# A second layer in twelve rounds per head pair, with the last block's projections spread over its eight periods

## The chip, the cores and the metric

The kernel runs on one core of a Trainium2 chip. The time is the device time of one execution in microseconds. TensorE (PE) does the matrix products, VectorE (DVE), ScalarE (ACT) and GpSimd (POOL) the elementwise work, SyncE (SP) issues all DMAs here.

## What is computed

One step of a two-layer encoder on 2048 prompt tokens and 8 running streams of 16 tokens, model width 1024, in fp32. Layer 1 is a gated delta rule; layer 2, which the change concerns, is RWKV-7 time mixing with 16 heads of 64. The core of layer 2 in the reference:

```python
xs = h[None] + xx[None] * mu[:, None, None, :]
rkvz = jnp.einsum('gbtd,dge->gbte', xs[:4], w_in.reshape(D, 4, W_B)).astype(f32)
r, k, v, z = rkvz[0], rkvz[1], rkvz[2], rkvz[3]
def step(S, inp):
    r_t, w_t, k_t, v_t, a_t, b_t = inp
    sa = jnp.einsum('bhvk,bhk->bhv', S, a_t)
    S = S * w_t[:, :, None, :] + sa[..., None] * b_t[:, :, None, :] + v_t[..., None] * k_t[:, :, None, :]
    return S, jnp.einsum('bhvk,bhk->bhv', S, r_t)
```

The scan's output is normalised per head, a bonus term (the sum of r k r_k, times v) is added, it is multiplied by the SiLU gate of z and goes through the output projection; a last RMSNorm follows. Both layers start with an RMSNorm.

## The kernel before

**Tiling.** Layer 2 has six blocks (`B_BLOCKS`): the first of two 64-token chunks and the 8 x 16 sample tokens, then five of 384 tokens, which are six chunks. A block has eight head pairs (`KT`), so there are 48 pairs. Head pairs are handled in 54 **periods**: period i takes pair i through its preparation, and earlier pairs through later stages.

**Stages of a pair**, each a Python generator whose `yield` ends a step:

- `b_prep` (period i): two low-rank products (L1050), the elementwise work on DVE, ACT and POOL, the key norms (L1114), the bonus product (L1123, kept in `bv`), the masked chunk products (L1138, masked by DVE at L1143 into `GM`), and at the end `N`, written to DRAM (`scrb`) and read back as `B`.
- `b_subst` (period i + 1): a forward substitution of 15 steps of two small DVE instructions each (L776, L778), then two transfers through DRAM (`sc2b`, `cm`).
- `b_inverse` (period i + 2): POOL spreads `cm` into T (L1195), then products L1211 (three times), L1225, L1240, L106, L1259, and L1272 with L1275; T is updated between them by DVE, ACT and POOL.
- `b_scan` (period i + 3): for each chunk a product px (L1309), copied to `XV` by ACT (L1312, L1313); then L1316, the product pu (L1320), and L1325. DVE makes the next chunk's XV from pu (L1322) and the state R (L1323). So L1309 of a chunk needs L1322 of the one before. Sample tokens have products of their own (L1339 to L1364). `b_centre` subtracts the mean into `OC`.
- `b_gate` (in the period of the scan): group norm of OC (POOL scales it at L1402), a turn of OC by PE (L106, a helper's line), bonus and SiLU gate on DVE (L1411, L1412), and the split into `oh` and `ol` (L162, L163).
- `b_out` (every other period, for two pairs): eight output products of six matmuls each (L168 to L170) with weights `whl` from DRAM in two buffers. `b_final` is the last norm of a block (`norm_scale`, L204 and L205).

**The stream.** Beside the pairs a generator `b_stream` computes the projections of the blocks, one block and more ahead: 136 **units** per block, each of six 128 x 384 matmuls (L991 to L993) with one weight pair (six buffers, loaded at L133). Results go to DRAM (`kvd`), and `b_load` fetches K, R and V of a pair. A period takes `PACE` = 17 units; 101 were taken ahead of the first period, so that the stream ends in period 43, and periods 44 to 53 have no unit.

**What sets the order.** PE's instructions stand in the order in which the code is recorded (`MANUAL`). In a period `weave` sets it: each part has a number of steps and a stretch (a, b) of the period, and the part whose next step lies earliest goes on. The other engines' queues and SyncE's are sorted by a scheduler after due times that are taken from PE's order (`_due`).

```python
parts.append((self.b_scan(*at(i - 3)), 16, 0.1, 0.8))
parts.append((self.b_subst(*at(i - 1)), 15, 0.0, 0.55))
parts.append((self.b_gate(*at(i - 3)), 4, 0.7, 1.0))
parts.append((islice(st, PACE), PACE, 0.0, 1.0))
```

## Time and profile before

| | |
|---|---|
| median of three runs (lowest to highest) | 4778.23 us (4771.09 to 4779.44) |
| the profiled execution | 4774.21 us, its span 4772.5 us |
| busy share of the span | PE 93%, PE's weight loads 79%, DVE 72%, ACT 48%, POOL 36% |
| granted TensorE clock over the span | 0.954 of full speed |
| layer 2, from its first L1050 to the end | 2498 to 4772.5 us |
| first pair of blocks 1 and 2 | L1050 at 2806 and 3198 us |
| first pair of the last block | L1050 at 4340 us |

The table by stage gives for each stretch the busy time of each engine (with its number of instructions), the granted clock (PEclk, 1.00 is 2.4 GHz, 0.50 is 1.2 GHz), the DMA engines' share and GB/s. In a timeline, the brackets behind an instruction say how long its engine stood idle ahead of it and what ended that.

### The profile page before, as it was taken

What the parts mean: (1) busy time and instruction counts of PE and PEld (TensorE: products, weight loads), DVE (VectorE), ACT (ScalarE), POOL (GpSimd) and SP (SyncE); (2) the same over time, 40 slices, a digit from 0 to 9 for tenths busy, and PEclk for the clock granted to TensorE, in tenths of its full rate; (3) what the DMA queues carried; (4) which work ended last, traced back from release to release, by engine and by line L of the source; (5) the groups of instructions that cost most, each with busy time, mean ns of one, the idle gap of its engine ahead of it and who ended that gap; (6) DMA issues with size and microseconds to landing.
All of it is one profiled execution on the core that took longest, in us unless ns stands there. A gap on an engine that the chain in (4) does not pass through costs nothing.

```text
span 4772.5 us, 103994 instructions
## 1 busy us (share of the span) xinstructions
PE 4427.8 (93%) x37093; PEld 3776.5 (79%) x37093; DVE 3446.9 (72%) x9156; ACT 2307.5 (48%) x6197; POOL 1730.0 (36%) x2507
## 2 busy tenths in 40 slices
PE   6899999999999999999887988989999999999976
PEld 6778788878888899999886766878877877787765
DVE  5777866686666766766778888777776776777674
ACT  4544544454444444444475565554554454455442
POOL 5555443332111211111115454444443343343441
PEclk9999999999999999999998989999999999999987
DMA  6655665565555676676555666746656665665432
GB/s 196 193 178 184 214 214 176 171 190 174 155 142 158 177 210 178 190 217 182 167 174 171 221 203 208 223 145 197 193 168 182 175 189 169 174 196 154 129 85 63
DMA packets 767975, 845.33 MB, mean 177 GB/s; under 512 B 263736, under 2 KB 499664, under 8 KB 767456
## 3 DMA queue, kind: packets, MB, share of 16 engines
q1 hardware_dynamic: 767456, 838.68, 59.3%
q8 instruction: 293, 4.80, 0.4%
q14 instruction: 226, 1.85, 0.1%
HBM read 635.88 MB, written 202.53 MB: 176 GB/s over the span
## 4 chain that ended last, share of the span: by engine, by line
PE 64%; DVE 19%; ACT 5%; issue 4%; DMA 4%; POOL 3%; SPq 0%; POOLq 0%; DVEq 0%; ACTq 0%
PE ps L390 6%; PE ps L392 6%; PE ps L391 6%; PE ps L991 5%; PE ps L168 4%; PE ps L169 4%; PE ps L992 4%; PE ps L993 4%; PE ps L170 4%; DVE sbt L776 2%; DVE cv L505 2%; PE ps L1320 2%; DVE TB L778 2%; PE ps L1309 1%; PE ps L106 1%
## 5 line engine op out<-in xcount | busy, mean ns | idle before, releaser
L390 PE MATMUL ps<-hh,whl 128*128 128x384 f32 (+1 forms) x1960 | 798.4, 407 | 10.4 <-ACT hh L162 8.2
L392 PE MATMUL ps<-hh,whl 128*128 128x384 f32 (+1 forms) x1960 | 715.2, 365 | 3.5 <-POOL whl L125 3.2
L391 PE MATMUL ps<-hl,whl 128*128 128x384 f32 (+1 forms) x1960 | 712.5, 364 | 1.8 <-DVE hl L163 1.5
L991 PE MATMUL ps<-xh,whl 128*128 128x384 f32 (+1 forms) x1632 | 623.7, 382 | 15.0 <-ACT whl L124 7.0
L992 PE MATMUL ps<-xl,whl 128*128 128x384 f32 (+1 forms) x1632 | 557.3, 341 | 17.3 <-POOL xl L163 12.7
L993 PE MATMUL ps<-xh,whl 128*128 128x384 f32 (+1 forms) x1632 | 555.2, 340 | 6.4 <-DVE whl L125 5.9
L125 POOL TENSOR_TENSOR whl<-wraw,whl 128x256 fp32r<-128x256 f32 x454 | 368.2, 816 | 416.9 <-ACT whl L124 390.7
L505 DVE SCALAR_TENSOR_TENSOR cv<-pre,cw,cv 128x512 f32<-128x512 f32 (+3 forms) x576 | 381.3, 669 | 137.2 <-ACT cv L503 130.9
L390 PEld LDWEIGHTS ps<-hh,whl 128*128 128x128 f32 x1960 | 375.5, 192 | 65.3 <-issue 16.4
L124 ACT CAST whl<-wraw 128x256 fp32r<-128x256 f32 x726 | 287.7, 404 | 261.4 <-PE ps L392 85.0
L392 PEld LDWEIGHTS ps<-hh,whl 128*128 128x128 f32 x1960 | 375.0, 191 | 41.8 <-POOL whl L125 7.2
L391 PEld LDWEIGHTS ps<-hl,whl 128*128 128x128 f32 x1960 | 376.1, 192 | 34.1 <-DVE hl L163 4.8
L168 PE MATMUL ps<-oh,whl 128*128 128x384 f32 (+2 forms) x1024 | 393.0, 384 | 9.4 <-ACT oh L162 4.1
L169 PE MATMUL ps<-ol,whl 128*128 128x384 f32 (+2 forms) x1024 | 366.3, 358 | 9.0 <-DVE ol L163 8.9
L991 PEld LDWEIGHTS ps<-xh,whl 128*128 128x128 f32 x1632 | 320.3, 196 | 64.6 <-ACT whl L124 8.5
L170 PE MATMUL ps<-oh,whl 128*128 128x384 f32 (+2 forms) x1024 | 364.4, 356 | 0.0
L778 DVE TENSOR_TENSOR TB<-TB,sbt 48x15 f32<-48x15 f32 (+14 forms) x1320 | 335.6, 254 | 19.7
L776 DVE TENSOR_TENSOR sbt<-B,TB 48x15 f32<-48x15 f32 (+14 forms) x1320 | 330.9, 251 | 25.2 <-DMA B<-scrb 3.2
L992 PEld LDWEIGHTS ps<-xl,whl 128*128 128x128 f32 x1632 | 322.5, 198 | 31.5 <-POOL xl L163 17.0
L993 PEld LDWEIGHTS ps<-xh,whl 128*128 128x128 f32 x1632 | 322.0, 197 | 10.9 <-DVE whl L125 10.4
L754 DVE TENSOR_TENSOR x<-x,ps 128x384 f32<-128x384 f32 (+1 forms) x320 | 191.2, 597 | 94.2 <-PE ps L170 91.2
L168 PEld LDWEIGHTS ps<-oh,whl 128*128 128x128 f32 x1024 | 199.2, 195 | 38.0 <-ACT oh L162 7.3
(342 smaller groups left out, 10365.4 us busy)
## 6 DMA issues: line engine op xcount, KB each, us to landing
whl<-wd SPq DMA_DIRECT2D x1582, 256.0 KB
wd<-whl SPq DMA_DIRECT2D x428, 256.0 KB
wraw<-in_w_a SPq DMA_DIRECT2D x288, 128.0 KB
wraw<-in_w_b SPq DMA_DIRECT2D x256, 128.0 KB
kvd<-kvo SPq DMA_DIRECT2D x160, 192.0 KB
xn<-x1d SPq DMA_DIRECT2D x80, 192.0 KB
wraw<-in_w_ao SPq DMA_DIRECT2D x96, 128.0 KB
xn<-in_x SPq DMA_DIRECT2D x48, 192.0 KB
```

Of the source, the lines that this page charges most:

```text
L168: self.nc.tensor.matmul(out, lhsT=wh, rhs=hh, start=first and i == 0, stop=False)
L169: self.nc.tensor.matmul(out, lhsT=wh, rhs=hl, start=False, stop=False)
L170: self.nc.tensor.matmul(out, lhsT=wl, rhs=hh, start=False, stop=i == n - 1)
L390: nc.tensor.matmul(p, lhsT=wh[:, k % 2], rhs=hh, start=k == 0, stop=False)
L391: nc.tensor.matmul(p, lhsT=wh[:, k % 2], rhs=hl, start=False, stop=False)
L392: nc.tensor.matmul(p, lhsT=wl[:, k % 2], rhs=hh, start=False, stop=k == KT - 1)
L505: nc.vector.scalar_tensor_tensor(o, f(j), self.cw[:, ct, j:j + 1], o, op0=MUL, op1=ADD)
L776: nc.vector.tensor_tensor(o, B[:, j + 1:16, j:j + 1].to_broadcast([rows, m, j + 1]), T[:, j:j + 1, 0:j + 1].to_broadcast([rows, m, j + 1]) ...
L778: nc.vector.tensor_tensor(T[:, j + 1:16, 0:j + 1], T[:, j + 1:16, 0:j + 1], o, op=SUB)
L991: nc.tensor.matmul(o, lhsT=wh[:, i], rhs=xh, start=k == 0, stop=False)
L992: nc.tensor.matmul(o, lhsT=wh[:, i], rhs=xl, start=False, stop=False)
L993: nc.tensor.matmul(o, lhsT=wl[:, i], rhs=xh, start=False, stop=k == KT - 1)
```

## The change

It replaces `weave` in layer 2 by `rounds`. A period has twelve rounds. Each part has a list of the rounds in which it makes a step, either written out or evenly spread over a stretch, and the parts are served in a fixed order in each round: prep, inverse, gate, substitution, scan, output products, last norm, stream. The scan makes one step in each round where it has twelve (2 per chunk, 6 for the sample tokens of the first block, spread over the period). The substitution takes rounds 1 to 8. The gate moves from the scan's period to the next one, rounds 1, 2, 3 and 6. The output products move to the second half of their period. `b_prep` has an empty step ahead of the norms and one ahead of the bonus product, and two fewer behind it. In the last eight periods of preparation (40 to 47) the stream takes 8 units (`LAST_PACE`) in place of 17. In `norm_scale` the mean square is taken from PSUM by one DVE instruction behind all products, where each column of up to three had its own. The `assert` lines add nothing to the program.

```diff
-AHEAD, PACE = 101, 17
+AHEAD, PACE, LAST_PACE, ROUNDS = 101, 17, 8, 12
...
                 nc.tensor.matmul(p1[0:w, c:c + 1], lhsT=acc[i][:, a:b], rhs=self.ones[:, 0:1], start=i == 0, stop=i == 1)
-            nc.vector.tensor_scalar(ms[0:w, 0, c:c + 1], p1[0:w, c:c + 1], 1.0 / D, 1e-6, op0=MUL, op1=ADD)
+        nc.vector.tensor_scalar(ms[:, 0, 0:len(spans)], p1[:, 0:len(spans)], 1.0 / D, 1e-6, op0=MUL, op1=ADD)
...
+    def rounds(n, parts):
+        live = []
+        for g, *at in parts:
+            if len(at) > 1:
+                k, a, e = at
+                at = [[max(1, math.ceil(n * (a + (e - a) * (i + 1) / k) - 1e-6)) for i in range(k)]]
+            live.append((g, list(at[0])))
+        for r in range(1, n + 1):
+            for p in list(live):
+                g, at = p
+                while p in live and ((at and at[0] <= r) or r == n):
+                    if at:
+                        at.pop(0)
+                    try:
+                        next(g)
+                    except StopIteration:
+                        live.remove(p)
...
+            if at(i):
+                parts.append((self.b_prep(*at(i)), range(1, 13)))
+            if at(i - 2):
+                parts.append((self.b_inverse(*at(i - 2)), (1, 2, 3, 4, 5, 6, 7, 8, 10)))
+            if at(i - 4):
+                parts.append((self.b_gate(*at(i - 4)), (1, 2, 3, 6)))
+            if at(i - 1):
+                parts.append((self.b_subst(*at(i - 1)), range(1, 9)))
             if at(i - 3):
-                parts.append((self.b_scan(*at(i - 3)), 16, 0.1, 0.8))
-            if at(i - 2):
-                parts.append((self.b_inverse(*at(i - 2)), 10, 0.0, 1.0))
+                b = at(i - 3)[0]
+                parts.append((self.b_scan(*at(i - 3)), 2 * b["ncp"] + 6 * b["nsc"], 0.0, 1.0))
...
-                    parts.append((out, 8, 0.0, 0.8))
+                    parts.append((out, 8, 0.5, 1.0))
                 else:
-                    parts.append((chain(out, self.b_final(blocks[j // KT])), 21, 0.0, 1.0))
+                    parts.append((chain(out, self.b_final(blocks[j // KT])), 21, 0.5, 1.0))
...
-            if at(i):
-                parts.append((self.b_prep(*at(i)), 12, 0.2 if i == 0 else 0.0, 1.0))
-            if at(i - 1):
-                parts.append((self.b_subst(*at(i - 1)), 15, 0.0, 0.55))
-            if at(i - 3):
-                parts.append((self.b_gate(*at(i - 3)), 4, 0.7, 1.0))
-            parts.append((islice(st, PACE), PACE, 0.0, 1.0))
-            self.weave(parts)
+            m = PACE if i < npair - KT else LAST_PACE
+            parts.append((islice(st, m), m, 0.0, 1.0))
+            self.rounds(ROUNDS, parts)
```

The lines of the changed kernel are shifted: L1309, L1316, L1320 and L1325 are L1334, L1341, L1345 and L1350, the units' L991 to L993 are L1014 to L1016, and L1211 is L1236.

**Scan and units.** PE's queue in period 28 (a middle block), from the scan's first pu product to the next chunk's px; before:

```order
L1316 MATMUL ps_49553<-R_30427,KR_47550 64x64 x2
L1320 MATMUL ps_49608<-XV_48884,TM_48883 64x64 x2
L1325 MATMUL ps_49553<-XV_48884,GM_47945 64x64 x2
L991 MATMUL ps_49404<-xh_49105,whl_49424 128x384
L992 MATMUL ps_49404<-xl_49106,whl_49424 128x384
L993 MATMUL ps_49404<-xh_49105,whl_49424 128x384
L991 MATMUL ps_49404<-xh_49112,whl_49424 128x384
L992 MATMUL ps_49404<-xl_49113,whl_49424 128x384
L993 MATMUL ps_49404<-xh_49112,whl_49424 128x384
L1309 MATMUL ps_49665<-XV_48884,GM_47945 64x64 x2
```

The same place in the changed kernel, where pu is in round 2 and the next px in round 3:

```order
L1341 MATMUL ps_49472<-R_30414,KR_47433 64x64 x2
L1345 MATMUL ps_49525<-XV_48781,TM_48780 64x64 x2
L1350 MATMUL ps_49472<-XV_48781,GM_47839 64x64 x2
L1014 MATMUL ps_49351<-xh_48922,whl_49313 128x384
L1015 MATMUL ps_49351<-xl_48923,whl_49313 128x384
L1016 MATMUL ps_49351<-xh_48922,whl_49313 128x384
L1014 MATMUL ps_49351<-xh_48929,whl_49313 128x384
L1015 MATMUL ps_49351<-xl_48930,whl_49313 128x384
L1016 MATMUL ps_49351<-xh_48929,whl_49313 128x384
L1236 MATMUL ps_49573<-Z_49440,T_49436 64x64 x12
L1236 MATMUL ps_49586<-T_49436,Z_49440 64x64 x12
L1334 MATMUL ps_49607<-XV_48781,GM_47839 64x64 x2
```

The inverse's 24 small products, which stood behind the px, now stand ahead of it.

**Output products.** PE's queue in period 29, where pairs 24 and 25 go through the output projection; before, the end of one step and what follows it (the next step comes after a px and 24 products L1211):

```order
L168 MATMUL ps_50311<-oh_50103,whl_50215 128x384
L169 MATMUL ps_50311<-ol_50104,whl_50215 128x384
L170 MATMUL ps_50311<-oh_50103,whl_50215 128x384
L1316 MATMUL ps_50259<-R_30429,KR_48306 64x64 x2
L1320 MATMUL ps_50327<-XV_49583,TM_49582 64x64 x2
L1325 MATMUL ps_50259<-XV_49583,GM_48596 64x64 x2
L991 MATMUL ps_50014<-xh_49105,whl_50076 128x384
L992 MATMUL ps_50014<-xl_49106,whl_50076 128x384
L993 MATMUL ps_50014<-xh_49105,whl_50076 128x384
L991 MATMUL ps_50014<-xh_49112,whl_50076 128x384
L992 MATMUL ps_50014<-xl_49113,whl_50076 128x384
L993 MATMUL ps_50014<-xh_49112,whl_50076 128x384
```

In the changed kernel, round 12 of that period:

```order
L168 MATMUL ps_50770<-oh_49781,whl_50727 128x384
L169 MATMUL ps_50770<-ol_49782,whl_50727 128x384
L170 MATMUL ps_50770<-oh_49781,whl_50727 128x384
L168 MATMUL ps_50770<-oh_50459,whl_50727 128x384
L169 MATMUL ps_50770<-ol_50460,whl_50727 128x384
L170 MATMUL ps_50770<-oh_50459,whl_50727 128x384
L168 MATMUL ps_50778<-oh_49781,whl_50768 128x384
L169 MATMUL ps_50778<-ol_49782,whl_50768 128x384
L170 MATMUL ps_50778<-oh_49781,whl_50768 128x384
L168 MATMUL ps_50778<-oh_50459,whl_50768 128x384
L169 MATMUL ps_50778<-ol_50460,whl_50768 128x384
L170 MATMUL ps_50778<-oh_50459,whl_50768 128x384
```

The last two steps, with two weight pairs, now stand back to back.

**The last block.** PE's queue in period 46, from the first pu on; before, where no unit is left:

```order
L1316 MATMUL ps_61408<-R_30431,KR_59945 64x64 x2
L1320 MATMUL ps_61455<-XV_60926,TM_60925 64x64 x2
L1325 MATMUL ps_61408<-XV_60926,GM_60224 64x64 x2
L1309 MATMUL ps_61495<-XV_60926,GM_60224 64x64 x2
L1211 MATMUL ps_61508<-Z_61381,T_61377 64x64 x12
L1211 MATMUL ps_61521<-T_61377,Z_61381 64x64 x12
```

and in the changed kernel:

```order
L1341 MATMUL ps_61266<-R_30418,KR_59578 64x64 x2
L1345 MATMUL ps_61307<-XV_60674,TM_60673 64x64 x2
L1350 MATMUL ps_61266<-XV_60674,GM_59868 64x64 x2
L1014 MATMUL ps_60788<-xh_59549,whl_60932 128x384
L1015 MATMUL ps_60788<-xl_59550,whl_60932 128x384
L1016 MATMUL ps_60788<-xh_59549,whl_60932 128x384
L1014 MATMUL ps_60788<-xh_59556,whl_60932 128x384
L1015 MATMUL ps_60788<-xl_59557,whl_60932 128x384
L1016 MATMUL ps_60788<-xh_59556,whl_60932 128x384
L1236 MATMUL ps_61354<-Z_61234,T_61230 64x64 x12
L1236 MATMUL ps_61367<-T_61230,Z_61234 64x64 x12
L1334 MATMUL ps_61388<-XV_60674,GM_59868 64x64 x2
```

A unit of the stream now stands between the scan's two products, as in the blocks before.

## Rows read from the trace of the kernel before

**Rows 1.** Busy time by stage of layer 2: stretch, length, engines, PEclk, DMA share, GB/s.

```profile
2498.00:2806.00 308.00, 265.74 (x2232) 216.44 (x2233) 263.53 (x817) 181.09 (x507) 160.21 (x244) 0.88 0.63 196
2806.00:3198.00 392.00, 353.17 (x3752) 287.50 (x3751) 313.73 (x837) 210.99 (x568) 186.52 (x234) 0.95 0.65 198
3198.00:4340.00 1142.00, 1087.72 (x12206) 910.53 (x12205) 841.31 (x2214) 577.30 (x1543) 467.81 (x573) 0.96 0.63 180
4340.00:4660.00 320.00, 281.34 (x3572) 230.70 (x3570) 227.17 (x643) 137.28 (x398) 134.00 (x168) 0.89 0.45 121
4660.00:4773.00 113.00, 76.03 (x883) 60.93 (x882) 50.45 (x143) 32.53 (x103) 18.49 (x21) 0.74 0.20 58
```

**Rows 2.** Waits of PE from 2498 to 4340: total us, times, longest.

```profile
PE ps L1309 <- DVE XV L1322: 34.3, 31, 2.0
PE ps L1211 <- POOL T L1195: 13.0, 3, 9.8
...
PE ps L169 <- DVE ol L163: 8.9, 10, 1.7
PE ps L106 <- POOL OC L1402: 8.2, 6, 2.0
PE ps L1351 <- DVE sbt L776: 6.7, 3, 3.2
...
PE ps L204 <- DVE nms L205: 4.4, 17, 0.4
PE ps L1123 <- DVE ch L1090: 3.9, 2, 2.1
PE ps L1320 <- ACT XV L1312: 3.9, 10, 0.8
```

**Rows 3.** PE's timeline in period 28: start, us, instruction, idle before.

```profile
3770.95 0.34 PE L1320 MATMUL ps<-XV,TM 128*64 128x64 f32 x4
...
3772.32 0.33 PE L993 MATMUL ps<-xh,whl 128*128 128x384 f32 x1
3774.41 0.74 PE L1309 MATMUL ps<-XV,GM 128*64 128x64 f32 x4 [1.76 <-DVE XV L1322]
```

**Rows 4.** DVE's timeline at the same place.

```profile
3771.76 1.32 DVE L1083 SCALAR_TENSOR_TENSOR ch<-ch,ch 128x384 f32<-128x384 f32 x1 [1.50 <-ACT ch L1081]
3773.11 0.94 DVE L1029 TENSOR_TENSOR w<-w2r,w 64x256 fp32r<-64x256 f32 x1
3774.08 0.60 DVE L1322 SCALAR_TENSOR_TENSOR XV<-ps,wc,Sw 64x64 f32<-64x64 f32 x2
```

**Rows 5.** PE's timeline at the end of a unit, without a wait.

```profile
3784.53 0.34 PE L992 MATMUL ps<-xl,whl 128*128 128x384 f32 x1
3784.71 0.34 PE L993 MATMUL ps<-xh,whl 128*128 128x384 f32 x1
3784.97 0.34 PE L1309 MATMUL ps<-XV,GM 128*64 128x64 f32 x4
```

**Rows 6.** Busy time in two stretches of period 28.

```profile
3787.50:3791.90 4.40, 3.90 (x47) 3.47 (x46) 2.15 (x13) 1.46 (x5) 0.62 (x1) 1.00 0.40 118
3791.90:3802.10 10.20, 10.20 (x74) 8.49 (x74) 3.65 (x10) 2.23 (x8) 3.22 (x8) 0.50 0.36 87
```

**Rows 7.** Busy time in periods 42, 44 and 45 of the last block.

```profile
4434.00:4474.00 40.00, 38.35 (x481) 31.78 (x480) 26.39 (x76) 16.62 (x50) 16.31 (x21) 1.00 0.60 167
...
4515.00:4552.00 37.00, 31.98 (x417) 26.02 (x412) 25.04 (x79) 15.54 (x47) 17.47 (x22) 0.63 0.19 51
4552.00:4594.00 42.00, 31.26 (x420) 25.53 (x420) 32.39 (x86) 15.19 (x45) 20.19 (x25) 0.84 0.54 146
```

**Rows 8.** PE's timeline in the last period: an output step ends, the second after it.

```profile
4745.58 0.34 PE L170 MATMUL ps<-oh,whl 128*128 128x384 f32 x1
...
4748.77 0.41 PE L168 MATMUL ps<-oh,whl 128*128 128x384 f32 x1 [0.97 <-DMA whl<-wd]
```

**Rows 9.** Waits of SyncE's queue from 2498 to 4340.

```profile
SPq L133 <- PE ps L993: 303.4, 226, 4.9
```

More of the change, by code (lines that the diff above doesn't have):

```diff
@@ L240, in weave @@
                 live.remove(p)
+    @staticmethod
+    def rounds(n, parts):
[15 more added lines that the diff above has]
+                        live.remove(p)
     def layers(self):
@@ L1018, in b_keep @@
         nc.sync.dma_start(b["kv"][g, q], t)
+        b.setdefault("kept", set()).add((g, q))
     def b_load(self, b, q):
@@ L1023, in b_load @@
             d[n] = self.mp.tile([P, b["NT"]], F32, name=self.nm(n), tag="kv" + n, bufs=bufs)
+            assert (g, q) in b["kept"]
             self.nc.sync.dma_start(d[n], b["kv"][g, q])
@@ L1109, in b_prep @@
         yield
+        yield
         pn = self.ps("g")
@@ L1120, in b_prep @@
         yield
+        yield
         pbn = self.ps("g")
@@ L1125, in b_prep @@
         nc.vector.tensor_tensor(bv, pbn[:, 0:NT], V, op=MUL)
-        yield
-        yield
         yield
@@ L1395, in b_gate @@
         SZ = self.mp.tile([P, NT], F32, name=self.nm("SZ"), tag="kvZ", bufs=1)
+        assert (3, q) in b["kept"]
         nc.sync.dma_start(SZ, b["kv"][3, q])
```

## The prediction

> **What bounds the kernel now.** I read the table by stage first [rows 1]. Layer 2 runs from 2498 us to the end of the span at 4772.5. In its three middle blocks (3198 to 4340 us) TensorE (PE) is busy 1087.72 of 1142 us, VectorE (DVE) 841.31; before and after that DVE comes closer (263.53 of 308, 227.17 of 320). PE runs in the order of the code, so it bounds layer 2, in two ways: it stands idle, and it is granted the low clock. Idle (stretch less PE busy) is 42.3 + 38.8 + 54.3 = 135 us up to 4340, 38.7 from there to 4660, 37.0 at the end. What the clock takes is (1 - PEclk) times the stretch: 37 + 20 + 46 = 102 us up to 4340, 35 to 4660.
>
> Second, who PE waits for [rows 2]: most of all the first product of a scan chunk (L1309) for the state that DVE makes from the chunk before (L1322): 34.3 us in 31 waits. Third, one such place [rows 3, 4]. The product L1320 ends at 3771.29, one unit of the projections stands behind it, and L1309 could start near 3772.6. DVE has an L1083 of 1.32 us and an L1029 of 0.94 ahead of the two L1322, so L1309 starts at 3774.41. About one such wait comes per pair: where one unit alone lies between the two. Elsewhere in a period there is more.
>
> Fourth, the price of a change of tile size [rows 5]: inside a unit a matmul starts 0.18 us after the last, and the small tile behind a unit after 0.26. Fifth, the last block [rows 7]: at 4434 to 4474 PE is busy 38.35 of 40 us at full clock; once the projections have run out it is busy 31.98 of 37 and 31.26 of 42, with PEclk 0.63 and 0.84.
>
> **Part by part, in the profiled execution.** It took 4774.2 us with a span of 4772.5; the median of the three runs, 4778.2, is 4.0 above, and I add that at the end.
>
> *The scan over the whole period (A1).* By the order, at least a unit and two dozen small 64-wide tiles now stand between the first L1320 and its L1309: the cover goes from 1.5 to 2.9 us (a unit is six starts of 0.18). The least cover is now about 2.1 us, from round 6 to 7 (a unit and the bonus product). The wait is 1.1 us in the mean (34.3 / 31), and the cover grows by 1.4 or 0.6: 25 of 34.3 go. What is late next is the same DVE instruction behind others: bounds 0 and 34.3. L1320 behind L1309, so far back to back once or twice per period, gets 1.65 us or more: 3.9 go.
>
> *The gate one period later, the empty rounds in prep, one L205 (A2).* L106 waits for the scaled scan output OC: 8.2 us. The gate now begins in round 1 and turns OC in round 6: 8.2 go. Its load of SZ goes with it and has five rounds; OC has one buffer, which the next scan writes in round 12 only. The bonus product's wait (L1123, 3.9) gets two rounds more: it goes. The three L205 wrote and read one PSUM tile in turn with L204; as one instruction behind all products they leave PE no wait: 4.4 go. It also saves two small DVE instructions per norm, which nobody waits for. Samples: L1351 waits 6.7 us for DVE busy with the substitution, and the scan steps are now twice as far apart; I take half, 3.4, since DVE is just as full there.
>
> A is 25 + 3.9 + 8.2 + 3.9 + 4.4 + 3.4 = 49 us, bounds 15 and 62. L1211 (13.0) I leave: it belongs to the filling of the pipeline, and the substitution now ends later (round 8 of 12), with four rounds for its two transfers. L169 (8.9) I leave too: the gate's last step in round 6 is followed by the first output product in round 7, about as close as before.
>
> *Clock that comes back (B).* Up to 4340 us 102 us of clock stand against 135 of idle, 0.75 for each. But the low clock also came without a wait: at 3791.9 for 10.2 us, behind a stretch in which PE was busy 3.90 of 4.40 us with small tiles [rows 6]. So half: 49 x 0.75 x 0.5 = 18 us, bounds 0 and 37.
>
> *Fewer changes of tile size (C).* Counted in the order, 155 runs of large matmuls end per block before, 119 after, in blocks 2 to 4; in blocks 1 and 0 it is 31 and 11 fewer. 150 ends fewer at 0.08 to 0.09 us [rows 5] is 13 us.
>
> *The last block (D).* Of the 57 units that are left when it starts, 25 go from periods 40 to 43 to periods 44 to 47. The stage from 4340 to 4660 has 281.34 us of PE, 35 of them by the low clock: 246 of work at full clock. DVE's 227.17 us at the best share that it reaches in [rows 1], 0.86, need 264. So the stage takes from 264 to 320 us; with half the idle (19) and two thirds of the clock loss (22) left it takes 287. D is 32 us, bounds 56 and -8. The last 113 us have no projections before or after: nothing.
>
> *Output products in half the period (E).* A step is six matmuls with a weight pair in two buffers. In the second half of every other period two steps stand back to back in rounds 9 and 12, and from the end of a step to the second one after it there are, summed from the starts of the instructions between, 3.1, 3.7 and 4.7 us at the tight places, against 7.4 or more before. The same back to back can be seen at the end: a step ends at 4745.92 and the second after it starts at 4748.77, having waited 0.97 us for its weights [rows 8]: 2.85 us for the round trip, on DMA queues that stand nearly idle. In the busy blocks SyncE's queue adds waits: L133 behind L993 held it 303.4 us in 226 waits, 1.34 in the mean [rows 9]. Behind a waiting L133 stand the projections' weights, the kv stores and the loads of the next pair. With 2.85 nothing is late; with 4.2 it is 1.1 + 0.5 us in each of 23 periods, 37 us. I take 10, near the row that shows the thing itself.
>
> The sum: 49 + 18 + 13 + 32 - 10 = 102 us. 4774.2 - 102 = 4672; with 4 for the median **4676 us**, 2.1% faster.
>
> **Rivals.** *The waits form again.* DVE is busy 0.71 to 0.86 of the time up to 4660 us [rows 1], and between the substitution and the rest it has few holes; by the order and the starts between, T in the inverse is now needed 2.8 us after its products, before 5.0 to 6.4. Then half of A and B, a third of D and double E are left: 24 + 9 + 13 + 11 - 20 = 37, 4741 us. For it: DVE's share. Against it: most waits are a queue of two instructions, not a lack of time.
>
> *The thin last block stays at the low clock.* The row shows full clock at 17 units a period and 0.63 without any [rows 7]; eight lie between. At 0.75 for the whole stage 246 us of work take 328: D is -8 and the time 4716. For it, the 0.63; against it, 0.84 in a period with output products, which have no more large matmuls than eight units have. The Trainium skill (TensorE: Matmul & The Clock Gate, What's actually happening) says that the low clock is the default and that activity lifts it; the rows agree, and by that rule spreading the units is a risk, and the time 4716 rather than 4676.
>
> *Slower: the output weights come late.* One mechanism, at the output products of rounds 9 to 12. If SyncE is held as long as its longest wait on a projection, 4.9 us, the round trip is 7.7. At 6.2 the three places lack 3.1, 2.5 and 1.5 us, 7.1 in each of 23 periods: 163 us in place of 10, and 4829 us. It decides from 5.5 us on, where the lack eats the other gains (112 us). For it: SyncE's order is one queue. Against it: no such wait before 4660, and a mean of 1.34. The Trainium skill (DMA: Bandwidth & Descriptors, Anatomy of one DMA — SWDGE (gpsimd) path) says that a DMA's wait is held by the sequencer that issues it, ahead of the DMA engines; the waits of SyncE's queue agree, and by it this rival's 4829 us is possible although the DMA engines have room.
>
> *The order has no effect.* The waits on the way are only moved to other places and the time is 4774 to 4782. The order does show the moves, so this needs all terms to cancel.
>
> **How the numbers follow.** The forecast 0.52 (its own range 4630 to 4715), waits again 0.20, thin block 0.12, no effect 0.06, slower 0.10. Faster is 0.84. A measurement of this kernel can tell about 0.2%, 9 us, from no change. The range reaches from 4615 (A and D near their bounds) to 4765, and leaves out no effect, slower, and the far end of the forecast.
>
> **What would show it.** A: in the changed profile L1309's line (now L1334) waits under 15 us for DVE up to the last block, L106 for OC nothing but at the end, L204 nothing for L205. B: PEclk 0.97 or more in the middle blocks, where a block takes about 365 us instead of 381. D: periods 40 to 47 in 280 to 295 us. E: waits of L168 for weights under 15 us before the last period. The forecast is wrong if the middle blocks take more than 375 us, if a new wait of over 30 us stands in the list (T, the gate's output, the weights), or if the last block is at PEclk 0.8 or less.

## The result, and the profile of the changed kernel

| | before | changed |
|---|---|---|
| median, us | 4778.83 | 4662.01 |
| runs, us | 4771.09 to 4781.03 | 4659.02 to 4668.1 |
| ratio, 95% interval | 1 | 0.976 [0.9743, 0.9777] |
| profiled execution (its span) | 4774.2 (4772.5) | 4660.79 (4659.1) |
| from the start of layer 2 to the last block | 1842.2 | 1771.2 |
| periods 40 to 47 | 320.0 | 280.6 |
| behind them | 112.5 | 105.4 |

The changed kernel is 2.4% faster, 14 us below the 4676 that were forecast. All medians below are of executions at the usual clock; two of the nine of e_group, an experiment further down (4897 and 5529 us, with a mean clock of 0.85 and 0.70) are left out. The profile's stages first, which answer to [rows 1]: stretch, its length, then busy time (and instructions) of PE, its weight loads, DVE, ACT and POOL, the mean granted clock of PE, the share of the DMA engines, GB/s. This is the busy time by stage, changed kernel.

```profile
2502.00:2806.00 304.00, 261.48 (x2234) 213.17 (x2235) 260.60 (x803) 181.38 (x506) 155.21 (x241) 0.89 0.62 196
2806.00:3175.00 369.00, 337.40 (x3742) 281.94 (x3741) 314.03 (x845) 209.53 (x569) 185.54 (x235) 0.95 0.69 209
3175.00:4273.00 1098.00, 1028.59 (x12208) 879.55 (x12207) 853.11 (x2203) 573.10 (x1543) 477.63 (x576) 0.97 0.65 188
4273.00:4554.00 281.00, 258.95 (x3586) 214.76 (x3586) 232.99 (x640) 134.54 (x398) 136.44 (x171) 0.93 0.51 139
4554.00:4659.00 105.00, 69.43 (x905) 55.77 (x900) 50.22 (x143) 32.84 (x104) 17.19 (x19) 0.78 0.22 63
```

Look at the third row. A middle block takes 366 us instead of 381, as forecast. But PE's idle time there is 1098 - 1028.59 = 69 us; before it was 54. Up to the last block it is 42.5 + 31.6 + 69.4 = 143.5 us against 135.4. The idle time did not go, although 71 us went. What is shorter is PE's busy time, by 79 us: 13 of it is the clock, 66 is PE's own work at full clock. In the forecast these two stood at 18 and 13, and the waits at 49. The rest of this text finds out why.

PE's waits from 2502 to 4273 us in the changed kernel, which answer to [rows 2]: who waits, for whom, total us, times, longest.

```profile
PE ps L1334 <- DVE XV L1347: 29.1, 21, 2.6
PE ps L1014 <- ACT xh L162: 16.9, 14, 1.9
PE ps L1389 <- DVE VS L1360: 9.1, 6, 2.6
...
PE ps L168 <- DMA whl<-wd: 6.7, 7, 1.4
```

The second line's counterpart before:

```profile
PE ps L991 <- ACT xh L162: 2.0, 2, 1.1
```

The scan's wait (L1334 is the old L1309) went from 34.3 us in 31 to 29.1 in 21: it comes less often and lasts longer. The waits of L106 for OC and of L204 for L205 are gone, but others stand in their place: a projection (L1014, the old L991, with 2.0 before) for its rounded input 16.9, the samples' L1389 (0.9 before) for VS 9.1, the output products (L168, none before) for their weights 6.7.

Why the scan still waits can be seen in period 28, on DVE and then on PE:

```profile
3735.37 0.90 DVE L797 TENSOR_TENSOR sbt<-B,TB 48x48 f32<-48x48 f32 x1
3736.30 1.04 DVE L799 TENSOR_TENSOR TB<-TB,sbt 48x48 f32<-48x48 f32 x1
...
3738.00 0.59 DVE L1347 SCALAR_TENSOR_TENSOR XV<-ps,wc,Sw 64x64 f32<-64x64 f32 x2
```

```profile
3738.32 0.65 PE L1334 MATMUL ps<-XV,GM 128*64 128x64 f32 x4 [1.08 <-DVE XV L1347]
```

L797 and L799 are the substitution (L776 and L778 before). Five of its instructions stand one behind the other on DVE ahead of the L1347 that PE needs. In each of the 21 waits DVE has such instructions in the wait or the 1.5 us ahead of it; before, that was so in 17 of 31, and at the place of [rows 4] it was L1083 and L1029.

### The profile page after: what moved, and what is told of

Its sections match the earlier page's. It is cut to its first block, busy times and chain, and to the rows that moved or that the text cites. A ratio compares the mean times of both kernels' runs of the same rounds, so it can differ in the third digit from the quotient of the medians.

```text
span 4659.1 us, 104090 instructions
## 1 busy us (share of the span) xinstructions
PE 4323.0 (93%) x37093; PEld 3720.0 (80%) x37093; DVE 3455.4 (74%) x9122; ACT 2299.3 (49%) x6197; POOL 1731.6 (37%) x2507
## 5 line engine op out<-in xcount | busy, mean ns | idle before, releaser
L1014 PE MATMUL ps<-xh,whl 128*128 128x384 f32 (+1 forms) x1632 | 606.7, 372 | 34.5 <-ACT xh L162 19.5
L1016 PE MATMUL ps<-xh,whl 128*128 128x384 f32 (+1 forms) x1632 | 558.7, 342 | 9.6 <-DVE whl L125 9.2
L526 DVE SCALAR_TENSOR_TENSOR cv<-pre,cw,cv 128x512 f32<-128x512 f32 (+3 forms) x576 | 379.3, 665 | 143.5 <-ACT cv L524 137.8
L168 PE MATMUL ps<-oh,whl 128*128 128x384 f32 (+2 forms) x1024 | 392.4, 383 | 28.7 <-DMA whl<-wd 14.0
L1014 PEld LDWEIGHTS ps<-xh,whl 128*128 128x128 f32 x1632 | 321.4, 197 | 78.6 <-ACT xh L162 26.1
L799 DVE TENSOR_TENSOR TB<-TB,sbt 48x15 f32<-48x15 f32 (+14 forms) x1320 | 355.6, 269 | 20.2
L797 DVE TENSOR_TENSOR sbt<-B,TB 48x15 f32<-48x15 f32 (+14 forms) x1320 | 347.3, 263 | 22.1 <-DMA B<-scr 1.3
L1016 PEld LDWEIGHTS ps<-xh,whl 128*128 128x128 f32 x1632 | 323.3, 198 | 17.7 <-DVE whl L125 17.0
L168 PEld LDWEIGHTS ps<-oh,whl 128*128 128x128 f32 x1024 | 199.0, 194 | 67.3 <-ACT oh L162 10.7
```

Of the source, the lines that this page charges most:

```text
L168: self.nc.tensor.matmul(out, lhsT=wh, rhs=hh, start=first and i == 0, stop=False)
L526: nc.vector.scalar_tensor_tensor(o, f(j), self.cw[:, ct, j:j + 1], o, op0=MUL, op1=ADD)
L799: nc.vector.tensor_tensor(T[:, j + 1:16, 0:j + 1], T[:, j + 1:16, 0:j + 1], o, op=SUB)
L1014: nc.tensor.matmul(o, lhsT=wh[:, i], rhs=xh, start=k == 0, stop=False)
L1016: nc.tensor.matmul(o, lhsT=wl[:, i], rhs=xh, start=False, stop=k == KT - 1)
```

## The experiments

The experiments stand between two theories. **R**: the gain up to the last block is that fewer runs of large matmuls end (a run is a stretch of 128x128 matmuls, projections and output steps, between small tiles). **W**: it is waits that went. Two more came up on the way: **M**, that the merged L205 is worth more than its waits, and **P**, that the order of the other engines, which the scheduler (the planner, in the texts below) shifts with every edit, makes the difference.

For every kernel PE's time from the start of layer 2 to the start of the last block is split in three, all from the trace's records. *Idle* is time without a matmul. *Clock* is half of the busy time at the low level (1.2 GHz), what the low level took. *Own* is what is left: PE's work at full clock. *Ends* are counted in PE's order. The ratio is to the kernel before on the same chip.

| kernel | ends | length | own | clock | idle | ratio, 95% interval |
|---|---|---|---|---|---|---|
| before | 610 | 1842.2 | 1614.6 | 92.2 | 135.4 | 1 |
| changed | 452 | 1771.2 | 1548.9 | 78.8 | 143.5 | 0.976 [0.9743, 0.9777] |
| changed, again (e_after) | 452 | 1770.9 | 1548.8 | 77.6 | 144.5 | 0.9751 [0.9728, 0.9774] |
| e_split | 597 | 1797.7 | 1593.4 | 71.8 | 132.4 | 0.98 [0.9781, 0.9818] |
| e_pairs | 379 | 1823.7 | 1524.6 | 110.0 | 189.1 | 0.9847 [0.982, 0.9874] |
| e_group | 323 | 1874.7 | 1513.4 | 113.0 | 248.3 | 0.9959 [0.9945, 0.9973] |
| e_gate | 552 | 1845.7 | 1599.0 | 91.3 | 155.4 | 1.0026 [1.0014, 1.0038] |
| e_wide | 616 | 1840.2 | 1601.6 | 95.8 | 142.7 | 0.9975 [0.9964, 0.9986] |
| e_norm3 | 452 | 1791.3 | 1547.0 | 91.1 | 153.2 | 0.981 [0.9787, 0.9833] |
| e_norm1 | 610 | 1828.4 | 1619.0 | 68.9 | 140.5 | 0.9952 [0.9939, 0.9965] |
| e_pace17 | 452 | 1770.7 | 1549.1 | 80.0 | 141.6 | 0.9771 [0.975, 0.9793] |
| e_gspread | 552 | 1846.6 | 1596.3 | 101.9 | 148.4 | 0.9995 [0.9986, 1.0004] |
| e_slack290 | 452 | 1767.8 | 1549.0 | 63.0 | 155.7 | 0.9758 [0.9741, 0.9774] |
| e_slack320 | 452 | 1784.4 | 1550.4 | 75.8 | 158.2 | 0.9751 [0.9731, 0.9771] |

The changed kernel's first two rows show how well this repeats: own within 0.1 us, idle and clock within 1.2. The two SLACK kernels (explained further down), where only the order of the other engines differs, have own within 2 us of it as well, but idle 11 to 15 us higher and clock up to 16 lower. So own is the firm column; a difference of some 15 us in idle or clock alone, from one profile each, shows little.

### What the end of a run of large matmuls costs

**e_split**: in rounds with two units the second goes ahead of the scan's step instead of next to the first, so that 597 runs end instead of 452.

```
+            if i < npair - KT:
+                parts.append((islice(st, 5), (3, 5, 8, 10, 12)))
             if at(i - 3):
...
-            m = PACE if i < npair - KT else LAST_PACE
-            parts.append((islice(st, m), m, 0.0, 1.0))
+            if i < npair - KT:
+                parts.append((islice(st, 12), range(1, 13)))
+            else:
+                parts.append((islice(st, LAST_PACE), LAST_PACE, 0.0, 1.0))
```

> The changed kernel, but in the rounds of periods 0 to 39 that have two units of the stream, one stands ahead of the scan's step and one behind it. Distances between the scan's products stay as they are within a unit; the ends of runs of large matmuls (before a 64-wide or smaller tile) go from 452 to 597, near the 610 of the kernel before. Theory R (the gain up to the last block comes from fewer such ends, which cost about 0.25 us each, by the account of the two traces' middle blocks): 145 x 0.25 = 36 us slower than the changed kernel, about 4698 us, with PE busy up by that much and idle as it was. Theory W (the gain comes from waits that go, as predicted): the same waits are covered, 4655 to 4670 us.

Measured: 4684.48 us, ratio 0.98, some 20 us slower than the changed kernel (by the ratios 0.976 and 0.9751). PE's own time grew by 44.5 us for 145 ends: 0.31 us each. Idle fell by 11 to 12 and clock by 6 to 7. The scan's wait, 29.1 us in the changed kernel, is 9.1 here:

```profile
PE ps L1338 <- DVE XV L1351: 9.1, 12, 1.5
```

With a unit between more of the small steps there is less waiting for the state, though other waits stand in its place. Idle and clock alone would show little here, but of the 44.5 us only some 20 are in the time. R has the larger part, W a smaller one.

**e_pairs** and **e_group** go the other way: units two at a time in eight rounds and one in a ninth (379 ends), or three at a time in even rounds (323).

```
-            m = PACE if i < npair - KT else LAST_PACE
-            parts.append((islice(st, m), m, 0.0, 1.0))
+            if i < npair - KT:
+                parts.append((islice(st, PACE), (1, 1, 2, 2, 3, 3, 5, 5, 6, 6, 7, 7, 9, 9, 10, 10, 12)))
...
+                parts.append((islice(st, PACE), (2, 2, 2, 4, 4, 4, 6, 6, 6, 8, 8, 8, 10, 10, 10, 12, 12)))
+            else:
+                parts.append((islice(st, LAST_PACE), LAST_PACE, 0.0, 1.0))
```

> The changed kernel with the seventeen units of a period two at a time in eight rounds and one in a ninth, instead of in all twelve; the rounds 4, 8 and 11 have none. The ends of runs of large matmuls over the first five blocks fall from 452 to 379. R (0.25 to 0.31 us for an end, as the kernels with 597 and 323 ends showed for PE's own work): 18 to 23 us less PE work, and as much off the time if no wait grows. W (a round without a unit leaves its small steps nothing to wait behind): idle time grows as it did with 323 ends, 105 us for 129 ends fewer, so about 60 us here, and the kernel is 35 to 45 us slower. Between the two I take 10 us slower as likeliest, since three rounds of twelve are left without a unit where the kernel with 323 ends left six.

> The changed kernel, but in periods 0 to 39 the 17 units stand in the six even rounds, three at a time (two in the last). Ends of runs of large matmuls go from 452 to 323. Theory R: 129 x 0.25 = 32 us faster than the changed kernel, about 4630 us, unless waits for the inputs of the units, which are now used three at a time, take it back. Theory W: px in the odd rounds now has no unit behind it, so the wait of the pu product for XV returns (0 to 0.4 us in 240 places) while the cover of px behind pu grows; 4655 to 4690 us.

Measured: e_pairs 4709.23 us, 45 us slower than the changed kernel's 4663.96 on the same chip; e_group 4762.52 us, ratio 0.9959. Both theories missed e_group; for e_pairs the upper end of W's 35 to 45 us came out, not the value that I took. PE's own time did fall as R says, by 24 and 35.5 us for 73 and 129 ends (0.33 and 0.28 us each). But idle grew by 45 and 104 us and clock by 32 and 35. The waits of PE up to the last block, e_pairs first, show where.

```profile
PE ps L1391 <- DVE VS L1362: 36.7, 14, 3.9
PE ps L1336 <- DVE XV L1349: 32.1, 22, 3.8
PE ps L1267 <- DVE T L1261: 26.2, 14, 3.5
PE ps L168 <- DMA whl<-wd: 17.1, 16, 1.8
```

And e_group:

```profile
PE ps L1267 <- DVE sbt L797: 33.6, 7, 5.3
PE ps L168 <- DMA whl<-wd: 31.9, 19, 4.4
PE ps L1391 <- DVE VS L1362: 27.7, 8, 5.2
PE ps L1267 <- DVE T L1261: 25.4, 14, 4.9
```

In the changed kernel the inverse (L1265, here L1267) waits 3.2 us for T and sbt. The samples' product that waits for VS (L1389, here L1391) went from 9.1 to 36.7 and 27.7, the output weights from 6.7 to 17.1 and 31.9. The reading that fits is that a round without a unit leaves its small steps with nothing to stand behind. So an end of a run costs about 0.3 us, and a unit in each of the twelve rounds is also the cover of that round. The three kernels have more and fewer ends than the changed one, and all are slower.

Where the 0.3 us come from can be read in the changed kernel's timeline of PE: start, duration (which overlaps the next), instruction, count.

```profile
3754.35 0.34 PE L1334 MATMUL ps<-XV,GM 128*64 128x64 f32 x4
3754.62 0.44 PE L1014 MATMUL ps<-xh,whl 128*128 128x384 f32 x1
3754.90 0.33 PE L1015 MATMUL ps<-xl,whl 128*128 128x384 f32 x1
3755.07 0.34 PE L1016 MATMUL ps<-xh,whl 128*128 128x384 f32 x1
...
3755.60 0.33 PE L1016 MATMUL ps<-xh,whl 128*128 128x384 f32 x1
3755.86 0.33 PE L1297 MATMUL ps<-GM,T 64*64 64x64 f32 x4
```

Within the run a matmul starts 0.17 to 0.18 us after the last. The small tile behind it starts after 0.26, which is the 0.08 to 0.09 that the prediction counted [rows 5]. But the second matmul of the run also starts late, 0.28 after the first (3754.90 behind 3754.62), another 0.10. And from a small to a large matmul there are 0.158 us in the mean (452 such starts, 71.2 us, counted at full clock), against 0.037 from small to small (12492, 468.1 us), another 0.12. Together about 0.3. None of it is idle time: the profile calls PE busy throughout. The Trainium skill (TensorEngine Tiling (Array Packing), Key Properties) says that a change of tiling mode drains the engine. The trace agrees in that the change costs time, here these 0.3 us for going out and coming back; that it is a drain the trace does not show.

### The gate, the output steps and the scan under `weave`

**e_gate** is the kernel before with the gate a period later in its first half and the output steps in the second half; nothing else, and no rounds. **e_wide** is that with the scan spread over its whole period.

```
-            if at(i - 3):
-                parts.append((self.b_gate(*at(i - 3)), 4, 0.7, 1.0))
+            if at(i - 4):
+                parts.append((self.b_gate(*at(i - 4)), 4, 0.0, 0.5))
...
-                    parts.append((out, 8, 0.0, 0.8))
+                    parts.append((out, 8, 0.5, 1.0))
...
-                parts.append((self.b_scan(*at(i - 3)), 16, 0.1, 0.8))
+                b = at(i - 3)[0]
+                parts.append((self.b_scan(*at(i - 3)), 2 * b["ncp"] + 6 * b["nsc"] + 1, 0.0, 1.0))
```

> The kernel before, with the gate moved to the next period (its first half) and the output products to the second half of theirs; weave and everything else stay. Ends of runs of large matmuls go from 610 to 552 up to the last block. Theory R: 58 x 0.25 = 15 us faster than before, about 4763 us. Theory W: the 8 us of waits for OC go and the clock that hangs on them, 10 to 14 us faster, 4765 to 4769 us.

> As the kernel with the moved gate, and the scan's steps are spread over the whole period (2 per chunk, 6 for the samples, and the last) by weave, with the units still one by one. Ends of runs of large matmuls go up to 616. Theory R: 64 x 0.25 = 16 us slower than with the moved gate alone, about 4779 us. Theory W: with twice the distance between the scan's products most of the 34 us of waits for XV go, and what stands in the clock behind them: 30 to 45 us faster than with the moved gate alone, about 4725 us.

Measured: e_gate 4796.35 us, 0.26% slower than before, where both theories had it faster. Own fell by 15.6 us with 58 ends fewer (0.27 each), but idle grew by 20. L991 waits 18.1 us for ACT's rounding of its input and L1309 42.8 us:

```profile
PE ps L1309 <- DVE XV L1322: 42.8, 36, 2.3
PE ps L991 <- ACT xh L162: 18.1, 11, 3.2
```

The wait for xh, 2.0 before and 16.9 in the changed kernel, comes with this part of the change; whether the gate or the output steps bring it was not tried apart. e_wide is 25 us faster than e_gate: L1309 waits 36.8 us in 19 instead of 42.8 in 36, and though 64 more runs end, own is only 2.6 us longer. The starts from small to small show why: they take 478.1 us in place of 501.8. When two steps of the scan stand back to back, the second seems to wait a little without the profile listing a wait. In the kernel before, L1320 starts 0.40 us behind L1316, and ACT ends the XV that it reads only at 3785.58 and 3785.82; in e_wide L1321 starts 0.26 behind L1317 (the same two).

```profile
3785.24 0.33 PE L1316 MATMUL ps<-R,KR 64*64 64x64 f32 x4
3785.64 0.50 PE L1320 MATMUL ps<-XV,TM 128*64 128x64 f32 x3
```

```profile
3790.17 0.33 PE L1317 MATMUL ps<-R,KR 64*64 64x64 f32 x4
3790.43 0.34 PE L1321 MATMUL ps<-XV,TM 128*64 128x64 f32 x4
```

Up to the last block e_wide gains only 5.5 us on e_gate; by the two profiles 7.6 came in the last block (313.3 against 320.9), 9.2 behind it and 3 ahead of layer 2, which one profile each does not settle. W's 30 to 45 us did not come out, nor R's 16 us slower.

### The last block

**e_pace17** is the changed kernel with 17 units a period to the end; **e_gspread** is e_gate with eight units a period in the last block. The spread alone on the kernel before was not tried: with the gate in the scan's own period it would read projections that are not yet written.

```
-AHEAD, PACE, LAST_PACE, ROUNDS = 101, 17, 8, 12
+AHEAD, PACE, LAST_PACE, ROUNDS = 101, 17, 17, 12
```

```
+            m = PACE if i < npair - KT else 8
-            parts.append((islice(st, PACE), PACE, 0.0, 1.0))
+            parts.append((islice(st, m), m, 0.0, 1.0))
```

> The changed kernel with 17 units a period in the last block too, as before; its first 40 periods are the same. The last block was 39 us shorter than before with the change. If that comes from the units spread over its eight periods: 35 to 42 us slower than the changed kernel on the same chip, the last block at 315 to 322 us with PE idle for 35 us or more and the granted clock at 0.92 or less, though it has fewer ends of runs of large matmuls (63 instead of 70). If it comes from the rounds (the scan spread over the whole period, the output steps in the second half): under 15 us slower, with the last block under 295 us. By the theory that ends of runs are all that counts: 2 us faster.

> The kernel before with the gate a period later, the output steps in the second half, and eight units a period in the last block; no rounds, and the scan as before. Against the kernel with the first two alone (4796 us, ratio 1.0026, last block 320.9 us and end 114.5 us) the units of the last block are the only difference. By my sum (the spread is worth 32 us): 4760 to 4768, last block 285 to 295 us. By the changed kernel with 17 units there (10 us slower by the median, its last block 302 us against 281 to 291): 10 to 16 us faster than with the gate alone, 4780 to 4786, last block 305 to 312 us. By ends of runs (77 in place of 71 there): 2 us slower.

Measured: e_pace17 4674.36 us, 10 us slower than the changed kernel beside it (every run of the one is above every run of the other). e_gspread has a ratio of 0.9995 [0.9986, 1.0004] where e_gate had 1.0026 on another chip: 0.31%, 15 us, give or take 7 by the two intervals. The stretch of periods 40 to 47 in e_after, e_pace17, e_gspread and e_gate, columns as in the first table of stages:

```profile
4261.00:4552.00 291.00, 268.69 (x3580) 222.77 (x3580) 231.49 (x640) 134.90 (x398) 135.48 (x171) 0.89 0.48 135
```

```profile
4261.50:4563.50 302.00, 263.20 (x3577) 217.51 (x3576) 233.66 (x641) 136.75 (x399) 133.54 (x171) 0.90 0.47 129
```

```profile
4354.00:4663.30 309.30, 276.96 (x3580) 226.07 (x3578) 228.21 (x644) 136.88 (x399) 129.27 (x169) 0.90 0.45 126
```

```profile
4352.90:4673.80 320.90, 279.28 (x3571) 228.27 (x3570) 224.15 (x644) 137.41 (x398) 136.04 (x170) 0.88 0.44 120
```

Idle is 22, 39, 32 and 42 us. The spread is worth 10 to 15, mainly in idle time, in both orders, and not 32. Its own profile in the changed order is not good to better than 10: the same stretch took 280.6 us in the first profile and 291.0 in e_after. With 17 units the changed order already brings the block from 320.0 to 302 us. So the rest of the change has as large a part in this stage as the spread that was written for it.

### One operation of L205 instead of three

**e_norm3** is the changed kernel with L205 as it was; **e_norm1** is the kernel before with only L205 merged; **e_slack290** and **e_slack320** are the changed kernel with another planner constant, which moves hundreds of instructions on the other engines and none on PE.

```
-        nc.vector.tensor_scalar(ms[:, 0, 0:len(spans)], p1[:, 0:len(spans)], 1.0 / D, 1e-6, op0=MUL, op1=ADD)
+            nc.vector.tensor_scalar(ms[0:w, 0, c:c + 1], p1[0:w, c:c + 1], 1.0 / D, 1e-6, op0=MUL, op1=ADD)
```

```
-LEAD, LEAD_DMA, SLACK = 6, 40, 300
+LEAD, LEAD_DMA, SLACK = 6, 40, 290
```

The changed kernel itself ran beside e_norm3:

> The changed kernel itself, once more, beside the three that follow, so that differences of a few us are taken on one chip. Both theories: a ratio of 0.974 to 0.978 to the kernel before, as in its first measurement, and again a stretch from 2498 us to the last block that is shorter in PE's own work (by some 65 us) and not in idle time.

> The changed kernel with the three small operations of L205 as before instead of one. The waits L204 <- L205 of before (4.4 us in 17 waits) should come back. By the waits' own size: 4 to 5 us slower than the changed kernel on the same chip. If a wait given back here only moves to the next one, as the scan's waits did: within 2 us. The two kernels of the first call with one L205 reached layer 2 at 2490 us and the two with three at 2504 to 2507, so a third reading is 12 to 17 us slower, if that difference is this edit's.

> The kernel before with one change alone: L205 as one small operation in place of three. PE's order is that of before; on the other engines some hundreds of places differ (917 rows on DVE), since the planner numbers all recorded operations. The changed kernel with three operations was 28 us slower than with one. Theory M (the merge itself is worth that): about 28 us faster than before here too, half of it ahead of layer 2. Theory P (the shift in the planner's numbers, which puts other engines' work in another order, made the 28 us): anywhere within 20 us of before. By the waits L204 <- L205 alone (4.4 us): 4 to 5 us faster.

> The changed kernel with the planner's SLACK at 290 instead of 300: the same instructions and the same order on PE, but 999 rows on DVE, 399 on ACT and 200 on POOL stand elsewhere, about as many as the three operations of L205 moved. M: within 6 us of the changed kernel (ratio 0.974 to 0.977). P: off by 10 to 30 us to either side, slower more likely than faster.

> The changed kernel with SLACK at 320: as the one before, to the other side (734 rows on DVE, 341 on ACT and 154 on POOL stand elsewhere). M: within 6 us of the changed kernel. P: off by 10 to 30 us to either side; the two together show how far an order of the other engines alone moves this kernel.

Measured: e_after 4663.96 us; e_norm3 4692.2, that is 28 us slower, where its waits (4.4 us) gave 4 to 5. e_norm1 has a ratio of 0.9952: 23 us faster than before with PE's order untouched. The two SLACK kernels have 0.9758 [0.9741, 0.9774] and 0.9751 [0.9731, 0.9771], the changed kernel's own ratio, though about as many instructions stand elsewhere as in e_norm1 (999 and 734 rows of DVE's order, 917 there). The intervals leave room for some 10 us either way, not for 28. So P falls and M stands: one small DVE operation in place of three is worth 23 to 28 us, about a fifth of the whole change.

How is seen in one place. First the kernel before, PE's timeline at a norm in period 28: twelve one-column matmuls in three groups.

```profile
3788.61 0.61 PE L204 MATMUL ps<-ones,nacc 128*128 128x1 f32 x4
3789.47 0.61 PE L204 MATMUL ps<-ones,nacc 128*128 128x1 f32 x4 [0.25 <-DVE nms L205]
3790.33 0.60 PE L204 MATMUL ps<-ones,nacc 128*128 128x1 f32 x4 [0.25 <-DVE nms L205]
3790.80 0.42 PE L991 MATMUL ps<-xh,whl 128*128 128x384 f32 x1
```

The same place in e_norm1:

```profile
3772.94 1.50 PE L204 MATMUL ps<-ones,nacc 128*128 128x1 f32 x12
3774.30 0.42 PE L991 MATMUL ps<-xh,whl 128*128 128x384 f32 x1
```

From the first to the projection behind they take 2.19 us in the one and 1.36 in the other. Now the ten microseconds around five norms of the middle blocks, before and then e_norm1 (columns as in the stages; the clock is the third number from the end):

```profile
3408.00:3418.00 10.00, 9.43 (x107) 7.75 (x106) 3.93 (x19) 3.25 (x11) 2.05 (x4) 0.83 0.31 86
3667.50:3677.50 10.00, 9.50 (x98) 8.62 (x100) 5.48 (x13) 3.09 (x9) 3.90 (x5) 1.00 0.62 172
3787.50:3797.50 10.00, 9.49 (x104) 7.91 (x104) 3.56 (x17) 3.10 (x11) 2.05 (x4) 0.72 0.29 85
4047.00:4057.00 10.00, 9.50 (x75) 8.63 (x75) 5.33 (x12) 2.27 (x7) 3.67 (x5) 0.83 0.53 156
4169.50:4179.50 10.00, 9.50 (x105) 7.93 (x104) 3.61 (x17) 3.14 (x11) 2.05 (x4) 0.73 0.32 90
```

```profile
3397.00:3407.00 10.00, 9.93 (x120) 8.43 (x120) 5.16 (x20) 3.86 (x13) 2.58 (x6) 1.00 0.49 124
3652.50:3662.50 10.00, 10.00 (x109) 9.05 (x106) 5.56 (x12) 3.62 (x10) 3.91 (x5) 1.00 0.61 169
3772.00:3782.00 10.00, 9.93 (x124) 8.57 (x124) 5.17 (x19) 3.92 (x12) 2.58 (x6) 1.00 0.44 115
4026.00:4036.00 10.00, 10.00 (x106) 9.05 (x106) 5.77 (x12) 3.75 (x11) 4.08 (x6) 1.00 0.59 169
4148.00:4158.00 10.00, 9.93 (x126) 8.57 (x122) 5.14 (x19) 4.01 (x13) 2.58 (x6) 1.00 0.40 115
```

Behind two waits of a quarter of a microsecond among one-column matmuls PE goes on at the low level, in four of the five places: 0.72 to 0.83, against 1.00 five times. It is not so each time: at 3667.5 both waits stand too and the clock stays at 1.00. At the same five norms e_norm3 has 0.83 twice and 1.00 three times, e_after 1.00 five times. Over all 17 norms of an execution, layer 1's too (1 us ahead of each to 8 us behind it), PE is at the low level for 60 to 82 us in the five kernels with three operations, and for 20 to 41 us in the nine with one. Half of the difference, some 20 us, is time lost. For the whole stretch up to the last block, before and e_norm1:

```profile
2498.00:4340.00 1842.00, 1706.62 (x18186) 1414.47 (x18187) 1418.56 (x3867) 969.38 (x2617) 814.54 (x1050) 0.94 0.63 186
```

```profile
2486.50:4315.00 1828.50, 1687.96 (x18187) 1398.82 (x18188) 1417.58 (x3851) 969.07 (x2617) 809.44 (x1050) 0.96 0.64 188
```

Idle is 135.4 and 140.5 us, no less; the clock went from 0.94 to 0.96. In the table the clock takes 23 us less in e_norm1 than before, and idle and own 5 and 4 more; from e_after to e_norm3 it takes 13 more, idle 9 more and own 2 less. So the clock carries the larger part, and the 0.8 us by which each norm is shorter don't show in the sums. The rows sort themselves by it: with one operation the clock takes 63 to 80 us (e_pairs and e_group, with their waits, apart), with three 91 to 102. Some 10 us of the gain seem to be in layer 1, which the prediction had left at nothing: it ends at 2493 us in the mean of the nine profiles with one operation and at 2504 in that of the five with three. But the ranges overlap (2486.5 to 2507.9 and 2497.9 to 2507.5), so this is not settled. The Trainium skill (TensorE: Matmul & The Clock Gate, What's actually happening) says that the low clock is the default and that activity lifts it; the rows agree as far as they go. Whether the 0.5 us of waits or the longer stretch of one-column matmuls lets the clock fall is not separated here.

## Why the prediction was right, and where it was not

The total was right: 4662 against 4676 in 4615 to 4765, faster, with the middle blocks at 366 us and the last block at 280.6. But that the total came so close is luck. Up to the last block the terms were 49 + 18 + 13 - 10 = 70 us and 71 went, yet as 66 of PE's own time, 13 of clock and 8 of idle time more. The largest term was nothing; PE's own time, forecast at 13, made up for it.

- **A, waits that go: 49 us. Wrong.** Idle time up to the last block went up by 8 us. The step that failed is "25 of 34.3 go" and, behind it, that nothing new is late. The longer cover made the scan's waits rarer (31 to 21) but not shorter in sum (34.3 to 29.1); the test that I named, under 15 us, failed (29.1, and 8.4 more in the last block). What is late is still DVE, now with steps of the substitution ahead in all 21 waits. L106, L204 and L1320 did lose their waits and the bonus product kept 2.4 of 3.9, but L1014's wait for xh (2.0 to 16.9) came, with the gate's move or that of the output steps, as e_gate shows. This is the rival of waits that form again, for the idle part. What the wide scan gave instead stands in PE's busy time: about 24 us less from small tile to small tile in e_wide, where I looked at listed waits only.
- **A2, L205: 4.4 us. Mis-sized.** It measured 23 to 28. The wait was priced by its own length; the larger part of its price is the clock behind it.
- **B, clock: 18 us. Size right, cause wrong.** The clock's loss fell by 13 to 15 us. I tied it to half of the waits, because the low level at 3791.9 seemed to come without one [rows 6]. That stretch was 0.50 us idle, which is the two waits on L205 at 3789.47 and 3790.33; in e_norm1, without them, the clock at this norm stays at 1.00. With L205 undone the loss is 91.1 again, as before (92.2).
- **C, changes of tile size: 13 us. Mis-sized by more than three.** The count was right (150 foreseen, 158 counted up to the last block), the price was not: I took the late start behind a run, 0.08 to 0.09, and left out the late entry and the late second matmul. At 0.3 us it is 47, the largest single term: with the 24 of the scan it is 71, and covers the 66 us that PE's own time lost. Sorted by kind in the two traces, the starts into, within and out of runs take 38 us less at full clock and those from small tile to small tile 27 less, so the division between the two is good to some 10 us.
- **D, the last block: 32 us. Right as a stage, wrong as a cause.** 29 to 39 us went (291.1 and 280.6 for 320.0). The spread gives 10 to 15 of it; about 18 come with the rest of the change (320.0 to 302.0 with seventeen units). The thin block did not stay at the low clock: 0.93 and 0.89 with eight units a period, 0.90 with seventeen.
- **E, output weights: -10 us. Right by the length of its waits.** L168 waits 8.6 us for DMA in 12 waits up to the end of period 47, with 1.4 us at the longest, and the list of before has none. The rival of late weights has its mechanism (31.9 us in e_group), but it is far from deciding here.

Two slips in the sums change little. Two thirds of the 35 us of clock loss are 23, not 22, so the last block's stage is 288 and its term 32, as stated. And A and D at their bounds give 4639; with B at its bound as well it is 4620, near the 4615 stated.

Of the 117 us, then, 23 to 28 are the merged L205, 10 to 15 the spread, -12 the gate and the output steps alone, 25 the wide scan, and some 60 to 70 are left for the rounds if the parts add up. About 49 of these are ends of runs (616 in e_wide, 452 changed, at 0.3 us). What the last 15 to 20 are was not measured alone, and that the parts add up is assumed: the 25 of the wide scan stand for the most part in the last block and behind it, where the spread and the rounds work too.

## What to carry to other kernels

Count how often PE changes between large and small tiles, and price the whole way out and back from the starts in the timeline, since none of it is listed as a wait; but keep one large piece of work behind each chain of small steps. A short wait can cost more by the granted clock behind it than by its length: look at the stretch that follows. And when a sum of terms comes out, check the terms, since here one of 49 us was nothing and one of 13 was about 45.

## What was not expected of the hardware

- Going from large to small tiles and back costs PE 0.28 to 0.33 us (three kernels with 323, 379 and 597 ends, against the changed one's 452; 0.27 in e_gate against before), all of it counted as busy.
- Behind twelve one-column matmuls with two waits of 0.25 us the clock was lower in four of five places: 0.72 to 0.83 over 10 us in which PE is busy 9.4 to 9.5, against 1.00 in all five without the waits. In e_norm3, with the waits put back into the changed kernel, it was so in two of five.
- With PE's order fixed, seven hundred to a thousand rows of DVE's order in other places left the time where it was to within some 10 us (0.9758 and 0.9751, to 0.976 and 0.9751), while idle and clock in the profile moved by up to 16 us.
